# A decoder layer on one core: sample scores in four column groups, stacked rows for the compressed values, attention steps and tail without GpSimd

## The chip, the cores and the metric

The program runs on one core of a Trainium2 chip. The metric is the device time of one execution in microseconds (us), lower is better. Engines are named as in the profile: PE is TensorE (PEld its weight loads), DVE is VectorE, ACT is ScalarE, POOL is GpSimd, SP is SyncE, which issues most DMAs.

## The reference, cut to what matters

One layer of a hybrid decoder serves 256 prompt positions and 8 sample tokens together, so every linear has 264 columns. All is float32.

```python
h = rms_norm(x, norm_mix_pre)
q, kc, vc, ks, vs, kw, vw, gates, u = project(h, w_in, pos)     # rotary on the first 32 of 128 dims of q and of all keys
# three attention branches: compressed blocks, selected blocks, sliding window
kc_c, vc_c = compress(kc, *cmp_w[0]), compress(vc, *cmp_w[1])   # 15 blocks
p = masked_softmax(q @ kc_c.T * SCALE, mask);  o_cmp = p @ vc_c
o_sel, o_win = ...                                              # at this length: causal, over all keys
o = gates[..., 0:1] * o_cmp + gates[..., 1:2] * o_sel + gates[..., 2:3] * o_win
x = x + rms_norm(concat(o, pool_mix(u)) @ w_o, norm_mix_post)
x = x + rms_norm(relu(rms_norm(x, norm_mlp_pre) @ w_up) ** 2 @ w_down, norm_mlp_post)
```

The sample tokens attend to 256 cached positions each (8 sequences, paged cache rows and window rows) and to themselves.

## The kernel before, in words

Every weight matrix passes PE in three products: a weight and an activation are each split into a high part (rounded to the one-pass type, fp32r) and a low rest, and `linear` (matmul on L236) adds high x high, low x high and high x low. A weight chunk of 1 MB is loaded by SP, ACT rounds it in halves (`wh`, L195), DVE makes the rest (`wl`, L193), two halves ahead of their use. A linear runs as a series of steps; a step is six 264-column matmuls. `run` counts these steps on one clock, and the table `AT` says at which steps the parts of everything else (the named streams: rotary, scores, values, sample attention, norms) put their instructions between the linears' matmuls. So the order on every engine is written by hand, and each engine works its queue in that order.

The places that matter here lie in the second query projection (`z_q1`, steps 232 to 263) and in the first output linear (`o_pool`, from 264), up to step 333:

- `rope_part` (L500 to L503) turns the first 32 dims of two heads of a query group. `start_group` gives two of the four heads to DVE and two to POOL for the products of L501 and L503.
- `scores(g, i)` works a unit of one KV group and 128 queries: score matmuls (L805, plain fp32), a masked copy out of PSUM (L806), maxima, exponentials on ACT (L791), denominators times gates (L817 to L820), and the scaling of the three probability tiles (L824): compressed and selected ones on DVE, window ones on POOL.
- `values(g, i)` transposes the probabilities (L848) and multiplies them with the values: 128 rows at a time in three one-pass products (L208 to L210), the 16 rows of the compressed branch in one plain fp32 matmul (L841).
- `sample_attn` transposes the cached keys of each of 8 sequences (L943: four transposes for one branch and sequence), copies them out (L946 on DVE, L948 on ACT), and scores them. `score` (L932) issues two matmuls with 32 stationary columns each, one per KV group, for one branch of one sequence; they write different 32-row strips of the PSUM tile `pS`. The value product (L1002) puts eight such narrow matmuls together, over all four strips.
- `z_evac` (L490) empties the four PSUM banks of `z_q1`; `o_pool` uses these banks again, step by step.
- The tail, after the last matmul of `w_down`: squares are added up (L1175 to L1177), summed over partitions by PE (L1425), `rstd_of` takes the root in three pieces, and eight pieces of 128 x 512 outputs are formed (L1458 on DVE for six, L1451 on ACT with POOL's L1452 for two) and stored, 256 KB each; POOL also forms the sample rows.

PSUM banks for transposes and scores are two (`pmisc`, tile px), used in turn.

Of the kernel before, what the change touches and what calls it, by code (L numbers as in the profile page):

```python
# [35 lines left out]
AT = {'loads': [18], 'norm1': [31, 39, 40], 'rope_c': [38], 'rows0': [36, 37, 38, 43, 45, 48, 50, 52, 54, 58], 'heads0': [58, 59], 'rope_s': [64], 'out0': [81, 87, 92, 104], 'rows1': [106, 107, 108, 111, 114, 116, 119, 121, 124, 126], 'rope_w': [107], 'heads1': [126, 126], 'gates': [135, 136, 137, 139, 141, 142], 'v_rows': [137, 137, 143], 'out1': [161, 167, 171, 177, 178], 'diff0': [179, 180, 183, 185, 185, 186, 188], 'diff1': [204, 206, 208, 210, 212, 214, 216], 'rope_q00': [232], 'rope_q01': [230], 'scores00': [244, 244, 244, 244, 244, 244, 245, 245, 245, 245, 246], 'scores01': [243, 245, 248, 250, 250, 253, 253, 254, 255, 255, 255, 256, 257, 261], 'values00': [256, 258, 258, 258, 263, 266], 'rope_q10': [266], 'rope_q11': [264], 'values01': [265, 268, 272, 279, 279, 282, 286, 288, 291, 295], 'scores10': [279, 284, 286, 288, 290, 293, 295, 296, 299, 300, 303], 'sample': [271, 280, 280, 280, 280, 283, 285, 285, 285, 285, 286, 287, 290, 290, 290, 291, 292, 293, 294, 295, 296, 297, 298, 299, 300, 307, 311, 315, 316, 317, 319, 319, 320, 323, 323, 325, 325, 326], 'scores11': [305, 309, 310, 311, 313, 314, 315, 316, 318, 319, 320, 321, 323, 326], 'values10': [312, 319, 321, 324, 326, 327], 'values11': [327, 327, 328, 328, 329, 329, 330, 330, 331, 332], 'norm2': [424, 425, 426, 427, 428, 430, 431, 432, 435, 436, 437, 439, 440, 441, 442, 443, 447, 451, 451, 457, 459, 460, 461], 'y_rows': [456, 460, 464, 468, 472, 476, 479, 487], 'shift': [651, 655, 659, 663, 667, 671, 674, 678, 683]}  # L36
# [67 lines left out]
def nsa_pool_step(ctx: ExitStack, tc: tile.TileContext, ins, outs):  # L104
# [504 lines left out]
    def cmp_out(slot, w2s, ph):  # L609
# [156 lines left out]
    def scores(g, i, st):  # L766
# [55 lines left out]
        for j, e in enumerate((eS[:, :, 0:16], eS[:, :, 16:], eW)):  # L822
            eng = nc.gpsimd if j == 2 else nc.vector
            eng.tensor_tensor(e, e, den[:, 4 * j:4 * j + 4, None].to_broadcast([128, 4, e.shape[2]]), op=ALU.mult)  # L824

    def values(g, i, st):
        qs = slice(i * 128, (i + 1) * 128)
        eS, eW = st["eS"], st["eW"]
        parts = [(eS[:, :, 0:16], 16, [vcP[:, g, :]])]
# [15 lines left out]
        for j, (e, kw, _) in enumerate(parts):  # L845
# [22 lines left out]
    def sample_attn():  # L868
# [60 lines left out]
        def score(b, br, kt_):  # L929
            for g in range(2):  # L930
                p0 = 32 * (2 * br + g)
                nc.tensor.matmul(pS[p0:p0 + 32, 0:256], qm[:, g, 32 * b:32 * b + 32], kt_[:, g * 256:(g + 1) * 256],  # L932
                                 start=b == 0, stop=b == NB - 1)

        for b in range(NB):
            load()
            r = loaded[b]
# [422 lines left out]
    for fc in range(NFC):  # L1360
# [58 lines left out]
    parts = [acc2, last_squares(m2[:, KT - 1, :], sqs)]  # L1419
    sums = [(pacc("pP")[:, 0:1], lambda a: (a[:, 0:128], ones[:, 0:1])),  # L1420
            (pacc("pS")[:, 0:1], lambda a: (a[:, 128:256], ones[:, 0:1])),
            (pmain()[:, 0:NB], lambda a: (ones, a[:, SEQ:T]))]
# [68 lines left out]
```

## Time and profile before

| | |
|---|---|
| median of 3 runs | 1178.67 us (1178.59 to 1181.34) |
| the profiled execution's own time | 1180.37 us |
| its span, first to last instruction | 1178.6 us |
| PE busy | 1150.8 us (98%) |
| DVE, ACT, POOL busy | 689.2, 544.9, 127.9 us |
| moved by DMA | 212.09 MB, mean 180 GB/s |

The profile is of one execution. Times inside it are from the span's start. A busy PE is not a PE at its peak, since matmuls overlap: the granted clock and the distance between the starts of matmuls tell more.

### The profile page before, as it was taken

To read this page: it belongs to the slowest core of one execution; us is meant where nothing else is said; L and a number is where in the kernel's file an instruction comes from. 1 tells how busy PE (TensorE), PEld (TensorE's weight loads), DVE (VectorE), ACT (ScalarE), POOL (GpSimd) and SP (SyncE) were. 2 spreads that over 40 slices of the span, in tenths; PEclk is the share of its full clock that TensorE was granted. 3 is DMA by queue.
4 is the path that set the end of the run, shared out by engine and by line. 5 is a ranking of instruction groups with operands and counts; after the bars stand their busy time and mean duration, and the time that the engine had idled before them with its cause. 6 is when DMAs were issued, how large, how long until landed. Compare 5 with 4: busy or idle time off the path is not lost.

```text
span 1178.6 us, 22160 instructions
## 1 busy us (share of the span) xinstructions
PE 1150.8 (98%) x9303; PEld 1119.4 (95%) x9303; DVE 689.2 (58%) x970; ACT 544.9 (46%) x794; POOL 127.9 (11%) x130
## 2 busy tenths in 40 slices
PE   9999999999999999999999999999999999999996
PEld 8899999887879899999999999999999999999995
DVE  6767667874655776555445554545555445555555
ACT  6545434444446665443335543334453334444442
POOL 0121124220012464000000000000000000000211
PEclk9999999999999999999999999999999999999998
DMA  8866545445545458555555555555555555555542
GB/s 296 236 218 200 169 136 171 129 155 197 163 148 166 139 179 279 202 179 179 179 179 179 179 181 180 181 184 182 184 179 184 184 184 182 170 192 179 178 145 74
DMA packets 115789, 212.09 MB, mean 180 GB/s; under 512 B 7307, under 2 KB 23475, under 8 KB 115553
## 3 DMA queue, kind: packets, MB, share of 16 engines
q1 hardware_dynamic: 114297, 204.68, 53.4%
q0 software_dynamic: 672, 5.27, 1.3%
q8 instruction: 73, 1.20, 0.4%
q10 hardware_dynamic: 720, 0.72, 0.2%
q14 instruction: 27, 0.22, 0.1%
HBM read 206.77 MB, written 8.52 MB: 183 GB/s over the span
## 4 chain that ended last, share of the span: by engine, by line
PE 76%; DVE 3%; POOL 1%; ACT 1%; issue 1%; DVEq 0%; POOLq 0%; ACTq 0%
PE pm L236 71%; PE px L805 1%; PE pa L932 1%; PE px L943 1%; PE px L848 1%; POOL acc L1162 1%; PE pa L1002 1%; DVE orow L1458 0%; POOL xT L1260 0%; PE pa L841 0%; PE px L1333 0%; DVE h2a L1268 0%; DVE eS L824 0%; PE pa L210 0%; PE pa L209 0%
## 5 line engine op out<-in xcount | busy, mean ns | idle before, releaser
L193 DVE TENSOR_TENSOR wl<-raw,wh 128x1024 fp32r<-128x1024 f32 (+1 forms) x355 | 434.5, 1225 | 359.6 <-ACT wh L195 358.6
L195 ACT ACTIVATE wh<-raw 128x1024 fp32r<-128x1024 f32 (+1 forms) x354 | 369.2, 1048 | 463.6 <-PE pm L236 413.9
L236 PE MATMUL pm<-ah,wh 128*128 128x264 f32 x1024 | 292.0, 285 | 0.0
L236 PE MATMUL pm<-al,wh 128*128 128x264 f32 x1024 | 291.1, 284 | 0.0
L236 PE MATMUL pm<-ah,wl 128*128 128x264 f32 x1024 | 291.0, 284 | 0.0
L236 PE MATMUL pm<-h2h,wh 128*128 128x264 f32 x992 | 283.6, 286 | 0.0
L236 PE MATMUL pm<-h2h,wl 128*128 128x264 f32 x992 | 282.5, 285 | 0.0
L236 PEld LDWEIGHTS pm<-ah,wh 128*128 128x128 f32 x1024 | 193.1, 189 | 0.0
L236 PEld LDWEIGHTS pm<-al,wh 128*128 128x128 f32 x1024 | 192.8, 188 | 0.0
L236 PEld LDWEIGHTS pm<-ah,wl 128*128 128x128 f32 x1024 | 192.3, 188 | 0.0
L236 PEld LDWEIGHTS pm<-h2h,wh 128*128 128x128 f32 x992 | 187.7, 189 | 0.4 <-ACT h2h L1263 0.4
L236 PEld LDWEIGHTS pm<-h2h,wl 128*128 128x128 f32 x992 | 186.9, 188 | 0.0
L236 PE MATMUL pm<-h2b,wh 128*128 128x264 f32 x496 | 141.1, 285 | 0.5 <-DVE h2b L1268 0.5
L236 PE MATMUL pm<-h2a,wh 128*128 128x264 f32 x496 | 141.0, 285 | 0.0
L236 PE MATMUL pm<-h_hi,wh 128*128 128x264 f32 x448 | 133.0, 297 | 1.7 <-ACT wh L195 0.7
L236 PE MATMUL pm<-h_hi,wl 128*128 128x264 f32 x448 | 127.7, 285 | 1.3 <-DVE wl L193 1.2
L236 PE MATMUL pm<-h_lo,wh 128*128 128x264 f32 x448 | 127.4, 286 | 0.5 <-DVE h_lo L385 0.5
L1162 POOL TENSOR_TENSOR acc<-acc,sq 128x264 f32<-128x264 f32 x42 | 38.8, 925 | 745.2 <-ACT sq L1158 742.9
L236 PEld LDWEIGHTS pm<-h2b,wh 128*128 128x128 f32 x496 | 93.4, 188 | 0.7 <-DVE h2b L1268 0.7
L236 PEld LDWEIGHTS pm<-h2a,wh 128*128 128x128 f32 x496 | 93.6, 189 | 0.1
L236 PEld LDWEIGHTS pm<-h_hi,wh 128*128 128x128 f32 x448 | 84.8, 189 | 4.3 <-ACT wh L195 1.3
L236 PEld LDWEIGHTS pm<-h_hi,wl 128*128 128x128 f32 x448 | 84.3, 188 | 1.9 <-DVE wl L193 1.9
(573 smaller groups left out, 1396.7 us busy)
## 6 DMA issues: line engine op xcount, KB each, us to landing
raw<-in_w_up SPq DMA_DIRECT2D x64, 1024.0 KB, 5.3
raw<-in_w_down SPq DMA_DIRECT2D x64, 1024.0 KB, 5.1
raw<-in_w_in SPq DMA_DIRECT2D x25, 1024.0 KB, 5.3
raw<-in_w_o SPq DMA_DIRECT2D x16, 1024.0 KB, 5.2
rows<-in_cache_kv SPq DMA_DIRECT2D x64, 128.0 KB, 4.5
out<-in_state_win_kv POOLq DMA_DIRECT2D x8, 510.0 KB, 10.6
raw<-in_w_in SPq DMA_DIRECT2D x5, 512.0 KB, 7.7
rows<-in_state_win_kv SPq DMA_DIRECT2D x8, 256.0 KB, 5.3
```

Of the source, the lines that this page charges most:

```text
L193: eng.tensor_tensor(wl[:, a_:b_], r[:, a_:b_], wh[:, a_:b_].bitcast(F32), op=ALU.subtract)
L195: nc.scalar.activation(wh[:, a_:b_], r[:, a_:b_], AF.Copy)
L236: nc.tensor.matmul(ps[m_][:, :T], w[:, k, m_ * 128:(m_ + 1) * 128], x[:, k0 + 2 * h + k, :], start=ci == 0 and h == 0 and k == 0 and p == ...
L805: nc.tensor.matmul(pv[:, h, :], zq[g][:, h0 + h, qs], kmat, start=True, stop=True)
L848: nc.tensor.transpose(pp[:kw, h * 128:(h + 1) * 128], e[:, h, :], ident)
L932: nc.tensor.matmul(pS[p0:p0 + 32, 0:256], qm[:, g, 32 * b:32 * b + 32], kt_[:, g * 256:(g + 1) * 256], start=b == 0, stop=b == NB - 1)
L943: nc.tensor.transpose(pp[:, o:o + 128], r[:, 2 * br + c, g * 128:(g + 1) * 128], ident)
L1002: nc.tensor.matmul(po[32 * a:32 * a + 32, :128], ptm[:, a, 32 * b:32 * b + 32], r[:, 2 * (b % 2) + br, g * 128:(g + 1) * 128], start=b == ...
L1162: nc.gpsimd.tensor_tensor(a, a, sq, op=ALU.add)
```

## The change

The scores of the sample: the two branches of a sequence are scored together, so `score` issues four narrow matmuls in a row, one per strip, 8 times instead of two matmuls 16 times. A third buffer holds the transposed keys. `ptm`, the zeroed tile for the value product, now takes over `qm`'s buffer after the last score instead of having its own.

The compressed values: their rows are stacked three times to 48, with high, low and high parts of the probabilities (`ec`, made by three small DVE operations) against high, high and low parts of the values (`vcP`), so that one one-pass matmul gives the three products. For this DVE copies `hx` three times side by side (`hx3`) ahead of the matmul that makes `vcP`.

POOL leaves the attention: all query rotary goes to DVE, and the selected and window probabilities are scaled by ACT, head by head (four ACTIVATEs for a tile). The table `AT` moves places in `z_q1` and `o_pool`. The tail has no POOL work: the sums go to one bank, the root is taken once, DVE forms all eight pieces and the sample rows, and the stores are issued from SP and ACT in turn.

```diff
-AT = {... 'diff1': [204, 206, 208, 210, 212, 214, 216], 'rope_q00': [232], 'rope_q01': [230], 'scores00': [244, 244, 244, 244, 244, 244, 245, 245, 245, 245, 246], ...
+AT = {... 'diff1': [204, 206, 208, 210, 212, 214, 217], 'rope_q00': [236], 'rope_q01': [230], 'scores00': [243, 243, 243, 243, 245, 245, 245, 246, 248, 248, 248], ...
...
+            hx3 = tp.tile([128, 2, 3, 16], F32, name="hx3", tag="hx3", bufs=1)
+            nc.vector.tensor_copy(hx3, hx[:, 256:288].rearrange("p (g c) -> p g c", g=2)[:, :, None, :]
+                                  .to_broadcast([128, 2, 3, 16]))
             po = pmisc()
             for i in range(2):
-                nc.tensor.matmul(po[:16, i * 128:(i + 1) * 128], hx[:, 256 + 16 * i:272 + 16 * i], w2s,
+                nc.tensor.matmul(po[:48, i * 128:(i + 1) * 128], hx3[:, i].rearrange("p r c -> p (r c)"), w2s,
                                  start=True, stop=True)
-            nc.vector.tensor_copy(vcP, po[:16, :256].rearrange("p (a d) -> p a d", a=2))
+            pv = po[:48, :256].rearrange("p (a d) -> p a d", a=2)
+            nc.scalar.activation(vcP, pv, AF.Copy)
+            nc.vector.tensor_tensor(vcP[32:48], pv[32:48], vcP[32:48].bitcast(F32), op=ALU.subtract)
...
         for j, e in enumerate((eS[:, :, 0:16], eS[:, :, 16:], eW)):
-            eng = nc.gpsimd if j == 2 else nc.vector
-            eng.tensor_tensor(e, e, den[:, 4 * j:4 * j + 4, None].to_broadcast([128, 4, e.shape[2]]), op=ALU.mult)
+            if j:
+                for h in range(4):
+                    c = 4 * j + h
+                    nc.scalar.activation(e[:, h, :], e[:, h, :], AF.Copy, scale=den[:, c:c + 1])
+            else:
+                nc.vector.tensor_tensor(e, e, den[:, 0:4, None].to_broadcast([128, 4, 16]), op=ALU.mult)
+            if j == 0:
+                ec = ap1.tile([128, 4, 48], F32R, name="ec", tag="ec")
+                st.update(ec=ec)
+                nc.vector.tensor_copy(ec[:, :, 0:16], e)
+                nc.vector.tensor_tensor(ec[:, :, 16:32], e, ec[:, :, 0:16].bitcast(F32), op=ALU.subtract)
+                nc.vector.tensor_copy(ec[:, :, 32:48], ec[:, :, 0:16].bitcast(F32))
...
-        def score(b, br, kt_):
-            for g in range(2):
-                p0 = 32 * (2 * br + g)
+        def score(b, kts):
+            for br, kt_ in enumerate(kts):
+                for g in range(2):
+                    p0 = 32 * (2 * br + g)
...
-                if pend:
+                kts.append(kt_)
+                if br == 0 and pend:
                     score(*pend)
-                pend = (b, br, kt_)
                 yield
+            pend = (b, kts)
...
-        for k, eng in enumerate((nc.vector, nc.gpsimd)):
-            start(f"rope_q{g}{k}", rope_part(zq[g][:32, 2 * k:2 * k + 2, :], swap, eng))
+        for k in range(2):
+            start(f"rope_q{g}{k}", rope_part(zq[g][:32, 2 * k:2 * k + 2, :], swap, nc.vector))
...
-    rstd_of(rr, [o for o, _ in sums])
+    nc.vector.tensor_scalar(m2[:, last, :], m2[:, last, :], g4[:, last:KT], None, op0=ALU.mult)
+    rstd_of(rr, ss[:, 0:10])
...
+            nc.vector.scalar_tensor_tensor(o, o if a < D - 512 else last_o[i], rr[:, i:i + 1], y,
+                                           op0=ALU.mult, op1=ALU.add)
+            (nc.scalar if i else nc.sync).dma_start(y_p[0, i * 128:(i + 1) * 128, a:b], o)
```

How the order moves at three places. First, DVE's queue at the start of `z_q1`: the rotary of the first query group (zq_188), the weight rests (wl) and the first masked copies of scores (eS). Before:

```order
L193 TENSOR_TENSOR wl<-raw,wh 128x1024
L500 STREAM_SHUFFLE sw<-zq_188 32x528
L501 TENSOR_TENSOR sw<-sw,cs 32x528
L502 TENSOR_TENSOR zq_188<-zq_188,cs 32x528
L503 TENSOR_TENSOR zq_188<-zq_188,sw 32x528
L500 STREAM_SHUFFLE sw<-zq_188 32x528
L502 TENSOR_TENSOR zq_188<-zq_188,cs 32x528
L193 TENSOR_TENSOR wl<-raw,wh 128x1024 x2
L806 TENSOR_TENSOR eS<-px,cs 128x272
```

and with the change:

```order
L501 TENSOR_TENSOR sw<-sw,cs 32x528
L502 TENSOR_TENSOR zq_188<-zq_188,cs 32x528
L503 TENSOR_TENSOR zq_188<-zq_188,sw 32x528
L193 TENSOR_TENSOR wl<-raw,wh 128x1024
L500 STREAM_SHUFFLE sw<-zq_188 32x528
L501 TENSOR_TENSOR sw<-sw,cs 32x528
L502 TENSOR_TENSOR zq_188<-zq_188,cs 32x528
L503 TENSOR_TENSOR zq_188<-zq_188,sw 32x528
L193 TENSOR_TENSOR wl<-raw,wh 128x1024
L812 TENSOR_TENSOR eS<-px,cs 128x2x144 x2
```

Both pairs of heads are now turned wholly on DVE, the second pair (heads 2 and 3) first, a weight rest between them and another before the first score is copied out.

Second, DVE's queue at the end of `z_q1`, where the query banks are emptied (zq_189) and the second unit's probabilities (eS) are scaled. Before:

```order
L490 TENSOR_TENSOR zq_189<-pm,rB 128x264 x2
L817 TENSOR_REDUCE den<-eS 128x4
L818 TENSOR_SCALAR den<-den 128x12
L819 RECIPROCAL den<-den 128x12
L820 TENSOR_TENSOR den<-den,G 128x12
L824 TENSOR_TENSOR eS<-eS,den 128x4x16
L824 TENSOR_TENSOR eS<-eS,den 128x4x256
L490 TENSOR_TENSOR zq_189<-pm,rB 128x264 x2
```

and with the change:

```order
L490 TENSOR_TENSOR zq_189<-pm,rB 128x264 x2
L823 TENSOR_REDUCE den<-eS 128x4
L824 TENSOR_SCALAR den<-den 128x12
L825 RECIPROCAL den<-den 128x12
L826 TENSOR_TENSOR den<-den,G 128x12
L834 TENSOR_TENSOR eS<-eS,den 128x4x16
L839 CAST ec<-eS 128x4x16
L840 TENSOR_TENSOR ec<-eS,ec 128x4x16
L841 CAST ec<-ec 128x4x16
L490 TENSOR_TENSOR zq_189<-pm,rB 128x264
```

The wide product (4 x 256) is gone from between the emptying of the first two banks and of the third; three products or copies of 4 x 16 stand in its place.

Third, PE's queue at one place of the sample scores in `o_pool`, all between two steps of the linear. Before:

```order
L943 MATMUL px<-cs,rows 128x128 x4
L932 MATMUL pa<-kt__3370,qm 32x256 x2
L943 MATMUL px<-cs,rows 128x128 x4
L932 MATMUL pa<-kt__3428,qm 32x256 x2
L943 MATMUL px<-cs,rows 128x128 x4
L932 MATMUL pa<-kt__3437,qm 32x256 x2
```

and with the change:

```order
L962 MATMUL px<-cs,rows 128x128 x4
L950 MATMUL pa<-kt__3363,qm 32x256 x2
L950 MATMUL pa<-kt__3374,qm 32x256 x2
L962 MATMUL px<-cs,rows 128x128 x8
L950 MATMUL pa<-kt__3432,qm 32x256 x2
L950 MATMUL pa<-kt__3443,qm 32x256 x2
```

The narrow matmuls now stand in fours, behind every second group of transposes.

## Rows read from the trace of the kernel before

**Rows 1.** The page: busy time and instructions of each engine.

```profile
PE 1150.8 (98%) x9303; PEld 1119.4 (95%) x9303; DVE 689.2 (58%) x970; ACT 544.9 (46%) x794; POOL 127.9 (11%) x130
```

**Rows 2.** Busy time by stretch: length, then PE, PEld, DVE, ACT, POOL, clock, DMA.

```profile
206.49:350.04 143.55, 138.93 (x1070) 116.79 (x1068) 95.31 (x172) 65.37 (x144) 18.30 (x12) 0.98 0.48 158
220.72:224.13 3.41, 3.41 (x17) 3.19 (x15) 2.41 (x7) 1.73 (x9) 0.00 (x0) 0.50 0.70 272
248.02:251.44 3.42, 3.42 (x15) 3.13 (x15) 3.18 (x6) 0.91 (x1) 2.07 (x2) 0.50 0.02 5
```

**Rows 3.** The chain of waits in attention: start, us, what (x2 per fp32 matmul).

```profile
290.64 0.44 PE px L943 x4
291.07 0.56 PE pa L932 x4
291.63 0.93 PE pm L236 x6
...
319.15 0.57 PE pa L1002 x16
319.73 0.92 PE pm L236 x6
...
328.28 1.05 PE pa L841 x2
...
345.05 0.44 PE px L848 x4
345.49 0.73 PE pm L236 x6
```

**Rows 4.** PE in order of time: one-pass value products of 512 columns.

```profile
337.37 0.40 PE L208 MATMUL pa<-th,vparts 128*128 128x512 f32 x1
337.60 0.40 PE L209 MATMUL pa<-tl,vparts 128*128 128x512 f32 x1
```

**Rows 5.** PE and DVE in order of time, first scores.

```profile
215.26 0.62 PE L805 MATMUL px<-kx,zq 128*128 128x272 f32 x2
219.85 0.76 PE L805 MATMUL px<-kx,zq 128*128 128x144 f32 x4 [2.75 <-POOL zq L503]
...
209.76 0.76 DVE L500 STREAM_SHUFFLE sw<-zq 32x528 f32<-32x528 f32 x1
212.64 0.75 DVE L500 STREAM_SHUFFLE sw<-zq 32x528 f32<-32x528 f32 x1
```

**Rows 6.** PE and DVE in order of time, end of the query projection.

```profile
247.13 0.39 PE L236 MATMUL pm<-cc_hi,wh 128*128 128x264 f32 x1 [1.88 <-DVE zq L490]
...
243.66 3.07 DVE L824 TENSOR_TENSOR eS<-eS,den 128x64 f32<-128x64 f32 x2
```

**Rows 7.** Groups of instructions: busy, mean ns of one, idle before.

```profile
L193 DVE TENSOR_TENSOR wl<-raw,wh 128x1024 fp32r<-128x1024 f32 (+1 forms) x355 | 434.5, 1225 | 359.6 <-ACT wh L195 358.6
L791 ACT ACTIVATE eW<-eW,nmx 128x256 f32<-128x256 f32 x8 | 4.0, 497 | 3.3 <-DVE nmx L780 3.3
```

**Rows 8.** DVE in order of time: a copy of transposed keys; then value rows (also PE).

```profile
287.27 0.69 DVE L946 COPY kt__3468<-px 128x512 f32<-128x512 f32 x1 [3.07 <-PE px L943]
...
164.55 0.42 DVE L638 COPY vcR<-px 128x256 f32<-128x256 f32 x1
...
163.78 0.61 PE L642 MATMUL px<-w2t,hx 128*16 128x128 f32 x4
```

**Rows 9.** The tail: chain of waits, DVE in order of time, one stretch.

```profile
1165.42 0.44 DVE sq L1176
...
1166.80 0.73 ACT rv L450 x3
...
1168.48 5.23 DVE L1458 SCALAR_TENSOR_TENSOR orow<-orow,rr,yrow 128x512 f32<-128x512 f32 x4
1173.63 1.40 DVE L1458 SCALAR_TENSOR_TENSOR orow<-pm,rr,yrow 128x512 f32<-128x512 f32 x2
...
1174.00:1176.50 2.50, 0.00 (x0) 0.00 (x0) 1.03 (x2) 0.00 (x0) 0.00 (x0) 0.50 1.02 367
```

More of the change, by code (lines that the diff above doesn't have):

```diff
@@ L541, in nsa_pool_step @@
     vcR = zp.tile([128, 2, 128], F32, name="vcR")
-    vcP = zp.tile([16, 2, 128], F32, name="vcP")
+    vcP = zp.tile([48, 2, 128], F32R, name="vcP")
     def split(dst_h, dst_l, src):
@@ L828, in values @@
         eS, eW = st["eS"], st["eW"]
-        parts = [(eS[:, :, 0:16], 16, [vcP[:, g, :]])]
+        parts = [(st["ec"].bitcast(F32), 48, [vcP[:, g, :]])]
         for k in range(i + 1):
@@ L967, in sample_attn @@
         score(*pend)
+        ptm = ap.tile([128, 4, 288], F32, name="ptm", tag="qm", bufs=1)
+        nc.gpsimd.memset(ptm, 0.0)
         pN = pmisc()
@@ L1411, in f @@
                         later(1, lambda: add_square(acc2, m2[:, j, :], j, sqs))
-                    later(2 if j < KT - 2 else 4, gain)
+                        later(2, gain)
             return f
@@ L1416, in nsa_pool_step @@
             run(linear(downs[fc][q], ah, al, d_evac(q)))
[L1419 to L1422, printed above, removed]
+    ss = pacc("pP")
+    rr = const.tile([128, 10], F32, name="rr")
+    last = KT - 1
+    sq15 = tq.tile([128, T], F32, name="sq", tag="sq", bufs=4)
+    nc.vector.tensor_tensor(sq15, m2[:, last, :], m2[:, last, :], op=ALU.mult)
+    parts = [acc2, *sqs, sq15]
     for k, a in enumerate(parts):
-        for o, f in sums:
-            nc.tensor.matmul(o, *f(a), start=k == 0, stop=k == len(parts) - 1)
+        end = k == len(parts) - 1
+        nc.tensor.matmul(ss[:, 0:1], a[:, 0:128], ones[:, 0:1], start=k == 0, stop=end, skip_group_check=True)
+        nc.tensor.matmul(ss[:, 1:2], a[:, 128:256], ones[:, 0:1], start=False, stop=end, skip_group_check=True)
+        nc.tensor.matmul(ss[:, 2:10], ones, a[:, SEQ:T], start=False, stop=end, skip_group_check=True)
     flush()
-    rr = const.tile([128, 10], F32, name="rr")
-    rstd_of(rr, [o for o, _ in sums])
+    nc.vector.tensor_scalar(m2[:, last, :], m2[:, last, :], g4[:, last:KT], None, op0=ALU.mult)
+    rstd_of(rr, ss[:, 0:10])
     last_o = [pmain(), pmain()]
@@ L1432, in nsa_pool_step @@
             nc.tensor.transpose(last_o[i][:, k * 128:(k + 1) * 128], m2[:, KT - 4 + k, i * 128:(i + 1) * 128], ident)
-    ts = tq.tile([128, KT, NB], F32, name="ts", tag="so", bufs=2)
-    nc.gpsimd.tensor_tensor(ts, m2[:, :, SEQ:T], rr[:, None, 2:10].to_broadcast([128, KT, NB]), op=ALU.mult)
-    tt = tq.tile([128, 128], F32, name="tt", tag="t_")
-    nc.gpsimd.tensor_tensor(tt.rearrange("p (t c) -> p c t", c=KT), ts, xT[:, :, SEQ:T], op=ALU.add)
-    pp = pmisc()
-    nc.tensor.transpose(pp[:, :128], tt, ident)
@@ L1439, in nsa_pool_step @@
-    os_ = tq.tile([128, 128], F32, name="os_", tag="so", bufs=2)
-    pieces = [(i, a, b) for a, b in ((0, 512), (512, 1024), (1024, 1536), (1536, 2048)) for i in range(2)]
-    pooled = [4, 5]
-    def piece(p):
-        i, a, b = pieces[p]
-        o, y = (rows[n][:, i, a:b] for n in "oy")
-        src = o if a < D - 512 else last_o[i][:, a - D + 512:b - D + 512]
-        return o, src, y, rr[:, i:i + 1], y_p[0, i * 128:(i + 1) * 128, a:b]
-    for p in pooled:
-        o, src, y, r, _ = piece(p)
-        nc.scalar.activation(o, src, AF.Copy, scale=r)
-        nc.gpsimd.tensor_tensor(o, o, y, op=ALU.add)
```

45 lines of the change are left out of this document (25 added, 20 removed).

## The prediction

> **What bounds it now.** Start with the page: PE is busy 98% of the span, every other engine far less [rows 1]. So time is gained only by giving PE less to do, by ending its idle moments, or by a shorter tail, where PE is nearly done. Next, the windows: the attention piece from 206.49 to 350.04 lasts 143.55 us with PE busy 138.93 of it at a mean granted clock of 0.98 [rows 2]. Inside it are two stretches of 3.4 us with clock 0.50, the 1.2 GHz level; the rest stands at 2.4 GHz. Then the list in order of time, for what came ahead of each stretch: PE had waited 2.75 us for POOL's rotary (L503) at 219.85 [rows 5], and 1.88 us for DVE's emptying of a bank (L490) at 247.13 [rows 6]. Last, the chain of waits, for what a part costs that stands between two steps of a linear [rows 3]: there the cost is from start to start, the next step included, and not the part's busy time.
>
> A step without neighbours takes 0.73 us (six matmuls at 345.49), and does so behind the transposes at 345.05 [rows 3]. That is my zero.
>
> **Fewer score groups.** Transposes, a pair of narrow score matmuls and the step behind them take 0.44 + 0.56 + 0.93 = 1.93 us at 290.64; without the pair, 0.44 + 0.73 = 1.17 [rows 3]. A pair costs 0.76 us, of which 0.20 falls on the step that follows it. Eight narrow matmuls in the value product, two rounds over all four strips, take 0.57 us and lengthen the next step to 0.92 [rows 3]. So four narrow ones should cost what two do now. Sixteen pairs become eight fours: 8 x 0.76 = 6.1, taken as **-6.0**. The ends: 0 if fours cost twice a pair, and -6.1. The Trainium skill, page "TensorEngine Tiling (Array Packing)", section Key Properties, says that switching the tiling mode drains TensorE. By that rule the lengthened step belongs to each group and the sum is the one above; by the group's own 0.56 us alone it would be -4.5. The 0.93 against 0.73 agrees with the rule.
>
> **Compressed values.** L841 is plain fp32 and takes 1.05 us at 328.28 [rows 3]. One-pass products of the same 512 columns start 0.23 us apart (337.37 and 337.60 [rows 4]). One each for four units: 4 x (1.05 - 0.23) = **-3.3**; the other end is 0, if the 48-row weight load and the mode cost as much as the passes. The three small operations that make `ec` are behind the denominators, on an engine that is 95.31 us busy of 143.55 [rows 2].
>
> **First wait.** It goes with its cause: POOL no longer turns heads. Two heads take DVE 212.64 - 209.76 = 2.88 us [rows 5]. In the new order DVE does heads 2 and 3, a weight rest (1.22 us [rows 7]), heads 0 and 1: 209.76 + 2.88 + 1.22 + 2.88 = 216.7, when PE reaches its first score at about 215.3 [rows 5]. That leaves a wait of 1.4, and I add 0.5 for a masked copy behind the next weight rest: 1.9 in place of 2.75. The stretch at half clock costs half its length, 1.7 us [rows 2]. Less idle, and that split in two, I take it as gone: -(2.75 - 1.9) - 1.7 = **-2.6**. Ends: -0.9 if the clock still falls, -4.4 if nothing waits.
>
> **Second wait.** The emptying L490 stands behind L824's wide product, 3.07 us at 243.66 [rows 6]. The change sends that to ACT; three 4 x 16 operations come in its place. PE's 1.88 us and the 1.7 of the half-clock stretch after it go: **-3.6**. The banks are then free under 1 us ahead of need, so the other end is 0.
>
> **Less cutting up.** The parts now stand at 54 places between steps, before at 59; places cost what a switch does, 0.1 each: **-0.5**, between 0 and -1.
>
> **Tail.** Three DVE operations ahead of the sums (0.44 each [rows 9]) become one: -0.8. The root's three pieces on ACT (0.73 us) become one: -0.4 at most, with DVE's later steps unchanged. DVE forms all eight pieces, 8 x 0.70 (half of the 1.40 for two without POOL beside them), and the sample rows 0.6: 6.2 us, where six took 5.23 + 1.40 = 6.6 with POOL beside them. The last piece, at 1175.0 so far, comes about 1.2 to 1.6 earlier. But the DMA engines are already at a share of 1.02 there, at 367 GB/s [rows 9]; 2.1 MB of output takes 5.7 us at that rate, so the stores cannot gain more than the first one does. **-1.3**, ends 0 and -1.6. The Trainium skill, page "Trainium Kernel Development and Optimization", section Key Constraints, says that DMAs issued from several engines run on the same 16 DMA engines, and several issuers only spare issue time. By it, sharing the stores between SP and ACT gains nothing itself; the share of 1.02 agrees, and I price it at nothing.
>
> **ACT's new work.** Each of 8 scaled tiles is four ACTIVATEs; the nearest row, 128 x 256, is 497 ns [rows 7]: 32 x 0.5 = 16 us, on an engine 65.37 us busy of 143.55 [rows 2]. I price it at nothing, as long as weight rounding (L195) stays two halves, that is 8 steps or 5.8 us, ahead. If that cover is gone it is rival E.
>
> **New waits.** `hx3` stands on DVE behind the copy of value rows (164.55 + 0.42), so it ends near 165.2, while PE came to L642 at 163.78 [rows 8]: +1.4. At one place of the scores (step 287) the transposes of three sequences now stand with no step between; two px banks are used in turn, each needs a copy of 0.69 us [rows 8] against 0.44 of transposes [rows 3]: +1.2 there and +0.3 at the next place. The low parts of the probabilities at step 280 stand behind two rotaries: +0.4. The last unit's 48-row transpose goes through ACT before its product: +0.3. Value rows are loaded closer together: +0.6. First transposes of each unit wait for ACT's scaling: +0.3. Together **+4.5**, between 0 (each estimate covered) and +8.
>
> **Sum.** -6.0 - 3.3 - 2.6 - 3.6 - 0.5 - 1.3 + 4.5 = -12.8. The profiled execution took 1180.37 us, 1.7 above the median of 1178.67; it would come to 1167.6, and the median to **1165.9 us**.
>
> **Rivals.**
> A, the forecast: 1165.9. Chance 0.64.
> B, the waits move and do not go. For: DVE gets POOL's rotary, and PE still waits 1.4 + 0.5 at the first score; the margin at the second place is under 1 us. Against: both causes leave. Without the 2.6 and 3.6 the sum is -6.6: 1172.1. Chance 0.20.
> C, no new waits: the estimates of +4.5 find cover in work that shifts earlier with the gains. Sum -17.3: 1161.4. Against: the wait at `hx3` is read from two rows. Chance 0.08.
> D, the change does not do what it says: fours do not run together, each costs two pairs. Without the 6.0, -6.8: 1171.9. For: no row shows scores of 256 columns on four strips. Against: the eight narrow matmuls in 0.57 us. Chance 0.04.
> E, slower. ACT works its queue in order, and two blocks of four ACTIVATEs per unit put 8 x 0.5 = 4 us ahead of a weight rounding; DVE's rest of it (1.22 us) follows. It decides when the rounding that PE needs next stands behind a block and less than 4 us ahead. Then PE loses about 3 us at each of four units and falls to half clock each time: 4 x (3 + 1.7) = 18.8, sum +6.0: 1184.7. Against: the lead of 5.8 us, and the idle before L193 is already put down to waiting for L195 [rows 7] with no loss on PE. Chance 0.04.
>
> **The numbers.** About 0.3%, 3.5 us, is what a measurement of this kernel can tell from no change. A, C and D lie beyond that on the fast side, and B in part: 6.6 less another miss of 3 is "same". So faster 0.90, same 0.06, slower 0.04. The range goes from 1161.0 (C) to 1172.5 (B and D, with some tenths); outside are E, deeper mixes of B and D, and the gain ends of several terms at once.
>
> **What would show it.** A group of four scores near 0.57 us and L858's product near 0.25 in PE's list; a wait of some 1.4 and 0.5 us at the first scores with no clock of 0.50 behind it; none at the end of the query projection; a wait of 1.4 us at the `vcP` product near 164; no POOL work in the attention; the last piece about 1.2 us earlier. The forecast is wrong if the stretches at 0.50 stay, if groups of four take 1.1 us, if ACT's scaling stands ahead of a rounding that PE waits for, or if new waits together pass 8 us.

## The result, and the profile after

| | before | changed |
|---|---|---|
| median, 6 runs each | 1180.57 us (1178.59 to 1181.70) | 1169.71 us (1168.04 to 1170.59) |
| ratio of the times | | 0.9909, 95% interval 0.9896 to 0.9922 |
| span of the profiled execution | 1178.6 us | 1167.7 us |

The change is faster by 10.7 us (9.2 to 12.3). The forecast was 12.8, and 1165.9 us in a range of 1161.0 to 1172.5; the time is inside it, 3.8 above the forecast, of which 1.9 is the base (1180.57 here, 1178.67 before).

Busy time of the engines in the changed kernel, the page's first part (before: [rows 1]):

```profile
PE 1142.2 (98%) x9311; PEld 1117.9 (96%) x9311; DVE 684.5 (59%) x982; ACT 554.2 (47%) x824; POOL 107.3 (9%) x118
```

PE is still the bound. The rest of the reading needs one ruler. Both kernels send the same 8256 matmuls of L236 through PE, so the time between the starts of two of them, counted in steps of six from the first, can be compared stretch by stretch:

| steps (us in the kernel before) | before | changed | difference |
|---|---|---|---|
| 146 to 150 (163 to 167): value rows | 4.17 | 5.60 | +1.43 |
| 203 to 293 (214 to 350): attention | 135.50 | 122.56 | -12.94 |
| 351 to 420: second norm | 68.30 | 69.56 | +1.26 |
| from the last one to the end: tail | 14.54 | 14.13 | -0.41 |

All other stretches differ by 0.2 in sum. Two of the four differences are partly the clock's. Attention before held two stretches at clock 0.50 [rows 2] and now holds none, -3.4; the one at 401.6 us before is gone, and another stands at 439.3 us now, behind a wait of 2.2 us for POOL's sum that stands in both kernels and had no fall behind it before; with no fall ahead of it, a wait of 1.1 us for `h2a` shows at 393.6, which is most of the +1.26. So without the falls attention went from 132.1 to 122.6, by 9.5 us. (The run with the new tail alone, further down, has the old attention and no fall in it: 132.43 us.)

What PE waits for in the attention of the changed kernel (the list of waits from 200 to 350 us: engine, tile and line, releaser, us in total, times, longest):

```profile
PE px L811 <- DVE zq L503: 1.2, 1, 1.2
PE px L962 <- DVE kt__3347 L965: 0.5, 1, 0.5
PE px L962 <- DMA rows<-in_cache_kv: 0.4, 1, 0.4
PE px L811 <- DVE eS L812: 0.3, 1, 0.3
PE pa L858 <- ACT th L868: 0.2, 1, 0.2
PE pa L1024 <- DVE ptm L1014: 0.2, 1, 0.2
```

The two waits of before (2.75 in [rows 5], 1.88 in [rows 6]) have become 1.2 and nothing, and five small ones, 1.6 together, are new. These are the forecast's 1.4, its 0.5 (here 0.3), and its list of new waits.

A place with one group of four scores, and one product of the stacked rows (PE in order of time):

```profile
278.42 0.60 PE L962 MATMUL px<-cs,rows 128*128 128x128 f32 x4
278.95 0.41 PE L950 MATMUL pa<-kt__3454,qm 128*32 128x256 f32 x2
278.96 0.41 PE L950 MATMUL pa<-kt__3471,qm 128*32 128x256 f32 x2
279.19 0.39 PE L950 MATMUL pa<-kt__3454,qm 128*32 128x256 f32 x2
279.20 0.39 PE L950 MATMUL pa<-kt__3471,qm 128*32 128x256 f32 x2
279.52 0.39 PE L236 MATMUL pm<-cc_hi,wh 128*128 128x264 f32 x1
...
235.78 0.50 PE L858 MATMUL pa<-th,vcP 48*128 48x512 f32 x1
236.21 0.66 PE L865 MATMUL px<-cs,eS 128*128 128x128 f32 x4
```

The four strips do run together: two matmuls start 10 ns apart, and the group takes 279.52 - 278.95 = 0.57 us, what the pair took [rows 3]. The stacked product takes 236.21 - 235.78 = 0.43 us from start to start, not the 0.23 that I had read from products of 128 rows [rows 4].

The copy of `hx` in the way of the `vcP` product (the chain of waits, 162 to 166 us):

```profile
162.00 2.35 DVE wl L193 x2
164.36 0.33 DVE vcR L638
164.69 0.13 DVE hx L642
```

and PE's own line:

```profile
164.95 0.61 PE L646 MATMUL px<-w2t,hx 128*48 128x128 f32 x4 [1.36 <-DVE hx L642]
```

PE had been free since 163.6, so it waits 1.36 us; the forecast said 1.4, from DVE's copy in [rows 8].

The tail (the chain of waits), and ahead of it the last linear matmul of the kernel before (PE in order of time):

```profile
1164.06 0.28 PE L236 MATMUL pm<-ah,wl 128*128 128x264 f32 x1
```

```profile
1153.90 0.13 PE pa L1451 x2
...
1156.32 0.45 PE pa L1453 x2
...
1156.79 0.28 ACT rv L450
...
1158.03 1.41 DVE orow L1464 x2
```

From the end of the linear at 1153.9 to the root's first step at 1156.79, 2.9 us, there is no wait: PE works through four parts with three sums each. Before there were two parts, the second after three DVE operations, and the root began at 1166.80 [rows 9], 2.5 us after the linear's end at 1164.34. The shorter root, 1.24 us to the first piece in place of 1.68 [rows 9], only makes up for that: the first output piece starts 4.1 us after the linear in both kernels. What DVE saved, PE now spends.

### The profile page after: what moved, and what is told of

Read it like the earlier page. It is cut to its first block, busy times and chain, and to the rows that moved or that the text cites. A ratio compares the mean times of both kernels' runs of the same rounds, so it can differ in the third digit from the quotient of the medians.

```text
span 1167.7 us, 22184 instructions
## 1 busy us (share of the span) xinstructions
PE 1142.2 (98%) x9311; PEld 1117.9 (96%) x9311; DVE 684.5 (59%) x982; ACT 554.2 (47%) x824; POOL 107.3 (9%) x118
## 4 chain that ended last, share of the span: by engine, by line
PE 87%; DVE 5%; DMA 3%; ACT 2%; issue 1%; POOL 1%; SPq 1%; DVEq 0%; ACTq 0%; POOLq 0%
PE pm L236 79%; DVE wl L193 2%; ACT wh L195 1%; DMA raw<-in_w_in 1%; PE pa L209 1%; PE pa L208 1%; PE pa L210 1%; PE px L811 1%; DMA rows<-in_cache_kv 1%; PE px L578 1%; PE px L962 1%; POOL acc L1182 1%; POOL xT L1280 1%; PE px L865 0%; DMA raw<-in_w_o 0%
## 5 line engine op out<-in xcount | busy, mean ns | idle before, releaser
L193 DVE TENSOR_TENSOR wl<-raw,wh 128x1024 fp32r<-128x1024 f32 (+1 forms) x355 | 434.0, 1223 | 363.4 <-ACT wh L195 362.6
L195 ACT ACTIVATE wh<-raw 128x1024 fp32r<-128x1024 f32 (+1 forms) x354 | 369.3, 1048 | 450.6 <-PE pm L236 413.3
L236 PE MATMUL pm<-ah,wh 128*128 128x264 f32 x1024 | 292.0, 285 | 0.0
L236 PE MATMUL pm<-al,wh 128*128 128x264 f32 x1024 | 291.1, 284 | 0.0
L236 PE MATMUL pm<-ah,wl 128*128 128x264 f32 x1024 | 291.0, 284 | 0.0
L236 PE MATMUL pm<-h2h,wh 128*128 128x264 f32 x992 | 283.6, 286 | 0.2 <-ACT h2h L1283 0.2
L236 PE MATMUL pm<-h2h,wl 128*128 128x264 f32 x992 | 282.6, 285 | 0.0
L236 PEld LDWEIGHTS pm<-ah,wh 128*128 128x128 f32 x1024 | 193.1, 189 | 0.0
L236 PEld LDWEIGHTS pm<-al,wh 128*128 128x128 f32 x1024 | 192.7, 188 | 0.0
L236 PEld LDWEIGHTS pm<-ah,wl 128*128 128x128 f32 x1024 | 192.3, 188 | 0.0
L236 PEld LDWEIGHTS pm<-h2h,wh 128*128 128x128 f32 x992 | 187.8, 189 | 0.5 <-ACT h2h L1283 0.5
L236 PEld LDWEIGHTS pm<-h2h,wl 128*128 128x128 f32 x992 | 187.1, 189 | 0.0
L236 PE MATMUL pm<-h2b,wh 128*128 128x264 f32 x496 | 141.9, 286 | 0.5 <-DVE h2b L1288 0.5
L236 PE MATMUL pm<-h2a,wh 128*128 128x264 f32 x496 | 140.6, 284 | 1.1 <-DVE h2a L1288 1.1
L236 PE MATMUL pm<-h_hi,wh 128*128 128x264 f32 x448 | 132.5, 296 | 1.1 <-DVE h_hi L426 0.5
L236 PE MATMUL pm<-h_hi,wl 128*128 128x264 f32 x448 | 127.5, 285 | 1.4 <-DVE wl L193 1.4
L236 PE MATMUL pm<-h_lo,wh 128*128 128x264 f32 x448 | 127.2, 285 | 0.5 <-DVE h_lo L385 0.5
L236 PEld LDWEIGHTS pm<-h2b,wh 128*128 128x128 f32 x496 | 94.1, 190 | 0.7 <-DVE h2b L1288 0.7
L236 PEld LDWEIGHTS pm<-h2a,wh 128*128 128x128 f32 x496 | 93.2, 188 | 1.3 <-DVE h2a L1288 1.3
L236 PEld LDWEIGHTS pm<-h_hi,wh 128*128 128x128 f32 x448 | 84.5, 189 | 3.5 <-ACT h_hi L381 0.7
L236 PEld LDWEIGHTS pm<-h_hi,wl 128*128 128x128 f32 x448 | 84.2, 188 | 2.0 <-DVE wl L193 2.0
```

Of the source, the lines that this page charges most:

```text
L193: eng.tensor_tensor(wl[:, a_:b_], r[:, a_:b_], wh[:, a_:b_].bitcast(F32), op=ALU.subtract)
L195: nc.scalar.activation(wh[:, a_:b_], r[:, a_:b_], AF.Copy)
L236: nc.tensor.matmul(ps[m_][:, :T], w[:, k, m_ * 128:(m_ + 1) * 128], x[:, k0 + 2 * h + k, :], start=ci == 0 and h == 0 and k == 0 and p == ...
```

## Experiments

Each kernel stands against the kernel before on the same chip, the difference in us being the ratio's on that median. Three groups: single parts in the kernel before, all parts or all places alone, and the changed kernel with one thing taken back. My theory after the result was the forecast's sum, with the falls of the clock set too high; the rivals were that the parts do not earn their price one by one, and that the places do.

**Score groups alone**, in the kernel before.

```diff
-                kt_ = ap1.tile([128, 512], F32, name="kt_", tag="pT", bufs=2)
+                kt_ = ap1.tile([128, 512], F32, name="kt_", tag="pT", bufs=3)
...
-                if pend:
+                kts.append(kt_)
+                if br == 0 and pend:
                     score(*pend)
```

> The kernel before with the score groups of four alone (third buffer for the transposed keys, ptm in qm's buffer), old places. My reading of the changed kernel's trace (group 0.57 us, neighbours as for a pair): 8 groups fewer at 0.76 us, -6.0 us, in a bound of -4.5 to -6. If four strips do not run together (rival D): 0 to +6 us. PE's list should show the group near 0.57 us and the step behind it 0.8 to 0.95.

Measured: 0.9953 (0.9937 to 0.9970), -5.5 us. Between steps 241 and 258, where all scores but the last stand, and free of falls in both, the kernel is 4.4 us shorter. Step by step: the six steps that lose a pair take 0.72 or 0.73 less each (1.92 to 1.20 in one), 4.35 in all. At the other two places three pairs became two fours with no step between them, and there one group less saves 0.5 and 0.3, not 0.72: 5.1 together. Waits of 0.5 for a copy and 0.3 for rows take 0.8 back. Another 1.3 us goes behind the scores, most of it in one step of the value product that waits for rows; that step takes 2.7 to 4.0 us in the six other traces with the old places and 4.35 here, so it is not shown to be the groups' doing. Rival D is out.

**Stacked rows alone.**

```diff
-    vcP = zp.tile([16, 2, 128], F32, name="vcP")
+    vcP = zp.tile([48, 2, 128], F32R, name="vcP")
...
+            if j == 0:
+                ec = ap1.tile([128, 4, 48], F32R, name="ec", tag="ec")
...
-        return ap1.tile([128, 2, T], F32, name="sw", tag="sw", bufs=1)[:32]
+        return ap1.tile([128, 2, T], F32, name="sw", tag="pT", bufs=2)[:32]
```

> The kernel before with the 48 stacked rows alone (hx3, ec, one-pass product), old places, GpSimd kept; the rotary's scratch tile shares the buffers of the transposed keys for space. By the prediction's prices: 4 x (1.05 - 0.23) less 1.4 for the wait on hx3 = -1.9 us. By the changed kernel's trace, where the product takes 0.43: 4 x (1.05 - 0.43) - 1.2 = -1.3 us. If the wait on hx3 does not show, -2.5 us.

Measured: 1.0052 (1.0035 to 1.0068), 6.1 us slower: no expectation had that sign. DVE and PE in order of time say why:

```profile
244.63 0.23 DVE L830 TENSOR_TENSOR eS<-eS,den 128x64 f32<-128x64 f32 x1
244.89 3.29 DVE L835 CAST ec<-eS 128x64 fp32r<-128x64 f32 x1
248.22 0.23 DVE L836 TENSOR_TENSOR ec<-eS,ec 128x64 fp32r<-128x64 f32 x1
248.37 0.19 DVE L837 CAST ec<-ec 128x64 fp32r<-128x64 f32 x1
...
248.70 1.02 PE L861 MATMUL px<-cs,ec 128*48 128x128 f32 x4 [3.47 <-DVE ec L837]
```

The same cast in the changed kernel:

```profile
227.86 0.20 DVE L839 CAST ec<-eS 128x64 fp32r<-128x64 f32 x1
```

A cast of 0.20 us took 3.29, and PE stood 3.47 us behind it. POOL, in the run with the stacked rows, was scaling the window probabilities and zeroing `qm` and `ptm` from 244.7 to 248.1:

```profile
244.73 1.90 POOL L830 TENSOR_TENSOR eW<-eW,den 128x1024 f32<-128x1024 f32 x1 [15.60 <-ACT wh L195]
246.57 0.58 POOL L1132 MEMSET qm<- 128x576 f32 x1
247.08 1.06 POOL L1134 MEMSET ptm<- 128x1152 f32 x1
```

DVE and POOL hold each other up, and the forecast had no term for it. The cast ends at 248.2, as POOL's last memset does. It was there to be read in the kernel before: DVE's L824 took 3.07 us [rows 6], beside this on POOL.

```profile
243.76 1.90 POOL L824 TENSOR_TENSOR eW<-eW,den 128x1024 f32<-128x1024 f32 x1 [15.12 <-ACT wh L195]
```

DVE's L824 is two products there, a short one and the wide one; the wide one began at 243.80, 0.04 us behind POOL's. In the run with the score groups it began at 243.37, 0.04 us ahead of POOL's, and DVE had the way (DVE, then POOL):

```profile
243.23 1.36 DVE L824 TENSOR_TENSOR eS<-eS,den 128x64 f32<-128x64 f32 x2
244.50 0.77 DVE L490 TENSOR_TENSOR zq<-pm,rB 128x264 f32<-128x264 f32 x2
245.19 2.23 DVE L193 TENSOR_TENSOR wl<-raw,wh 128x1024 fp32r<-128x1024 f32 x1
...
243.41 2.93 POOL L824 TENSOR_TENSOR eW<-eW,den 128x1024 f32<-128x1024 f32 x1 [14.84 <-ACT wh L195]
```

There L824 took 1.36, POOL 2.93 in place of 1.90, and PE's wait of 1.88 us was gone, though the edit touches neither L824 nor L490. So 1.9 of that run's -5.5 is this, and not the groups.

The Trainium skill, page "SBUF — State Buffer", section "Who interferes with whom", says that a VectorE instruction with two inputs in SBUF contends with a GpSimd instruction that reads SBUF, since they share a port pair, and that one holds it until it is done. By that rule the loser's time grows by what is left of the winner's, and the four rows agree to 0.2 us: 1.36 + 1.7 for DVE against POOL's 1.90, or 1.90 + 1.0 for POOL against the 1.2 that were left of DVE's product. Why the cast, which has one input, is held too, no row shows.

The product itself saves what its new length says: the four steps that hold it are 0.61 or 0.62 us shorter each than in the kernel before. The loss lies around it.

**POOL out of the attention alone**, in the kernel before.

```diff
-        for k, eng in enumerate((nc.vector, nc.gpsimd)):
+        for k in range(2):
...
-            eng = nc.gpsimd if j == 2 else nc.vector
+            if j:
+                for h in range(4):
+                    c = 4 * j + h
+                    nc.scalar.activation(e[:, h, :], e[:, h, :], AF.Copy, scale=den[:, c:c + 1])
```

> The kernel before with POOL out of the attention alone: rotary on DVE, selected and window probabilities scaled by ACT; old places, old scores, old values. If the engines alone end the two waits: -6.2 us (2.6 + 3.6) and no stretch at clock 0.50 near 220 and 248 us. If the places of the table are what ends them (the waits move to DVE's queue): between -2 and +2 us, with waits over 1.5 us left at the first scores. If ACT's blocks hold up the weight rounding: over +5 us.

Measured: 1.0035 (1.0020 to 1.0050), 4.1 us slower. Both old waits are gone: at the first scores PE waits 0.25 us for a copy and 0.54 for a weight rest, where it waited 2.75 for POOL. Others came. ACT, DVE and PE in order of time:

```profile
225.15 2.46 ACT L826 ACTIVATE eS<-eS,den 128x128 f32<-128x128 f32 x8 [0.77 <-DVE den L820]
227.51 1.99 ACT L195 ACTIVATE wh<-raw 128x1024 fp32r<-128x1024 f32 x2
...
228.59 1.23 DVE L193 TENSOR_TENSOR wl<-raw,wh 128x1024 fp32r<-128x1024 f32 x1 [3.27 <-ACT wh L195]
229.73 0.78 DVE L806 TENSOR_TENSOR eS<-px,cs 128x272 f32<-128x272 f32 x2
...
230.22 1.13 PE L805 MATMUL px<-zw,zq 128*128 128x256 f32 x4 [1.02 <-DVE eS L806]
```

ACT's block of eight stands ahead of the rounding (L195), DVE's rest of the weight (L193) waits 3.27 us for it, the score copies queue behind that, and PE waits for the copies. This is rival E's mechanism with another last link: not the weight, but the copy behind it. The same place in the changed kernel:

```profile
224.30 1.06 ACT L195 ACTIVATE wh<-raw 128x1024 fp32r<-128x1024 f32 x1 [1.09 <-issue]
...
225.39 1.23 DVE L193 TENSOR_TENSOR wl<-raw,wh 128x1024 fp32r<-128x1024 f32 x1 [0.72 <-ACT wh L195]
...
227.66 2.45 ACT L832 ACTIVATE eS<-eS,den 128x128 f32<-128x128 f32 x8 [0.76 <-DVE den L826]
```

A rounding and its rest stand ahead of the block, and nobody waits for what follows.

**Scaling on ACT alone** splits that run: of its diff the second part, the rotary left as before.

> The kernel before with the scaling of selected and window probabilities on ACT alone; rotary still on POOL, old places. It halves the run without GpSimd (+4.1 us). If ACT's blocks of 2.4 to 3.4 us ahead of a weight rounding are what cost there: +2 to +5 us, with DVE's L193 waiting over 2 us for L195 near 228 us and PE for DVE's score copies. If the moved rotary was the cost: -2 to -4 us, the wait at 245 us gone.

Measured: 1.0040 (1.0025 to 1.0055), 4.7 us slower, with PE waits of 1.6 and 1.4 for score copies and 1.4 for L193. So ACT's blocks, with what queues behind them, are the cost.

**Tail alone**: the last hunk of the change (the sums in one bank, L1446 on) in the kernel before.

> The kernel before with the new tail alone. By the prediction: -1.3 us, mostly because the root comes 0.8 us earlier. By the changed kernel's trace, where the first output piece starts as long after the last linear matmul as before (4.3 us) and the last store ends 0.4 us earlier by the same measure: -0.4 us. If the bytes of the stores set the end: 0.

Measured: 0.9996 (0.9984 to 1.0009), -0.5 us and not to be told from nothing. From the last matmul of the linears to the end it takes 13.87 us, 14.54 before.

**All parts in the old places**: the changed kernel with the old table.

```diff
-AT = {... 'rope_q00': [236], ... 'scores00': [243, 243, 243, 243, 245, ...
+AT = {... 'rope_q00': [232], ... 'scores00': [244, 244, 244, 244, 244, ...
```

> The changed kernel with the old table of places: all its parts, none of its new order. Against the kernel before: if the places are what lets the parts pay (the three parts measured alone sum to -5.5 + 6.1 + 4.1 = +5 us), 0 to +8 us, with waits of PE for DVE's copies and for the small probabilities as in those runs. If the parts help each other (no GpSimd, so no wide product between the parts of the stacked rows), -5 to -9 us.

Measured: 0.9986 (0.9972 to 1.0000), -1.7 us, between the two expectations. The single parts sum to -5.5 + 6.1 + 4.1 - 0.5 = +4.2; together they do better by 6. That is no sign that the parts help each other. The stacked rows' cast takes 0.20 us without POOL, but two of the single parts end the same wait, so that at step 225, where both stand, the single parts sum to -1.5 us and this run has -1.6 (each against the run with the new tail, which has the old attention and no fall in it). Much of the 6 is falls of the clock that the profiled runs of single parts had in the attention, 3.4 us by the ruler, and 2.1 in a step that waits for rows. PE still waits 2.8 us for score copies, 1.4 for window copies and 1.4 for DVE's rests of the output parts, the waits of the two runs with ACT's blocks in the old places.

**New places alone**: the same line the other way round, in the kernel before.

> The kernel before with the new table of places alone. If the new order is good in itself: -3 to -6 us. If it is cut to the new parts and does nothing for the old ones: -1 to +5 us, since POOL's rotary (L503, done at 219.8 us) and DVE's wide product are as late as before while the first scores now stand one step earlier.

Measured: 0.9988 (0.9978 to 0.9998), -1.4 us. The first scores still wait, 2.4 us. DVE, then POOL:

```profile
215.25 0.73 DVE L500 STREAM_SHUFFLE sw<-zq 32x528 f32<-32x528 f32 x1
...
210.92 2.91 POOL L501 TENSOR_TENSOR sw<-sw,cs 32x528 f32<-32x528 f32 x1 [8.37 <-issue]
213.90 1.31 POOL L503 TENSOR_TENSOR zq<-zq,sw 32x528 f32<-32x528 f32 x1
```

POOL's pair now comes first, and DVE's shuffle cannot start before POOL's L503 ends at 215.2, for there is one buffer for `sw`.

**Scratch copy earlier.** The changed kernel with `hx3` copied a step sooner:

```diff
         nc.vector.tensor_tensor(hx, hx, hu, op=ALU.mult)
+        if slot:
+            hx3 = tp.tile([128, 2, 3, 16], F32, name="hx3", tag="hx3", bufs=1)
+            nc.vector.tensor_copy(hx3, ...)
         yield
```

> The changed kernel with hx3 copied right behind the product that makes hx, a step earlier. The wait of 1.33 us at the vcP product near 164 us should go: 1.2 to 1.4 us less than the changed kernel, so -12 us against the kernel before. If another wait takes its place (w2 or the copy of value rows): no difference from the changed kernel, -10.7.

Measured: 0.9888 (0.9867 to 0.9908), -13.2 us. The interval overlaps the changed kernel's, but the trace has it plainly: steps 146 to 150 take 4.20 us again (5.60 in the changed kernel), with no wait at L646.

**The changed kernel without the stacked rows.**

```diff
-        parts = [(st["ec"].bitcast(F32), 48, [vcP[:, g, :]])]
+        parts = [(eS[:, :, 0:16], 16, [vcP[:, g, :]])]
```

> The changed kernel with the compressed values as before: 16 rows, the plain fp32 product, no hx3, no ec. By the prediction's terms the stacked rows earn 3.3 and cost 1.4 and 0.3: the run is 1.6 us slower than the changed kernel, -9.1 us against the kernel before. By the product's measured 0.43 us, they earn 2.5 and cost 1.3: 1.2 slower, -9.5. If they cost as much as in the run where they stood alone (+6.1), the run is faster than the changed kernel by some us, -13 or less.

Measured: 0.9899 (0.9877 to 0.9921), -11.9 us: not slower than the changed kernel, as far as can be measured. By the ruler it gains 1.41 us at steps 146 to 150 and loses 1.0 in the attention, where neither has a fall. The steps say more. The four that hold the product are 0.61 to 0.63 longer each, 2.5 in all (1.66 to 2.28 in the first). Against that two steps that wait for cached rows (256 and 285) are 0.65 and 0.66 shorter here. They vary without any change to the attention, too: in the run with the early copy they take 3.05 and 4.74, in the changed kernel 3.68 and 3.62. So the stacked rows earn 2.5 us at their products and pay 1.4 for `hx3`; whether the waits for rows are theirs as well, one trace does not tell.

**The changed kernel with POOL's half of the rotary.**

```diff
-            start(f"rope_q{g}{k}", rope_part(zq[g][:32, 2 * k:2 * k + 2, :], swap, nc.vector))
+            start(f"rope_q{g}{k}", rope_part(zq[g][:32, 2 * k:2 * k + 2, :], swap, eng))
```

> The changed kernel with the rotary of heads 2 and 3 of each group back on POOL. The prediction gave the move 0.85 us of wait and 1.7 of clock, 2.6 together: -8.1 us against the kernel before. If POOL's rotary was late only because of the old order: no difference, -10.7. If the new order, with the first scores a step earlier, is cut to DVE: 3 to 6 us slower than the changed kernel, with a wait over 2.5 us at the first scores.

Measured: 0.9907 (0.9885 to 0.9930), -11.0 us, no difference. PE, then DVE:

```profile
218.56 0.64 PE L811 MATMUL px<-kx,zq 128*128 128x144 f32 x3 [1.30 <-DVE zq L503]
...
215.96 1.82 DVE L502 TENSOR_TENSOR zq<-zq,cs 32x528 f32<-32x528 f32 x1
```

The wait at the first scores is 1.30 us, 1.17 in the changed kernel, although POOL turns two heads again: with three buffers for `sw` POOL and DVE overlap, and they slow each other (1.82 us where a lone one takes 0.69). So the wait of 2.75 came from POOL's pair standing second, behind DVE's queue and one buffer. There are two ways out of it: to take POOL out, as in the old places (0.25 and 0.54), or to put its pair first with three buffers (1.30). New places with one buffer (2.4) or two buffers in the old places (2.7, in the run with the stacked rows) do not end it.

**The changed kernel with the scaling as before.**

```diff
-            if j:
-                for h in range(4):
...
+            eng = nc.gpsimd if j == 2 else nc.vector
+            eng.tensor_tensor(e, e, den[:, 4 * j:4 * j + 4, None].to_broadcast([128, 4, e.shape[2]]), op=ALU.mult)
```

> The changed kernel with selected probabilities scaled by DVE and window ones by POOL, as before. The prediction gave this move 3.6 us: -7.1 us against the kernel before. In the old order ACT's scaling cost 4.7 us, so if the new order only takes that cost away: no difference, -10.7. If DVE's wide product and POOL's hold each other up again (DVE's 3.07 us at 243.7 against 1.36 in another run): a wait of 1.5 to 4 us at the end of the query projection, and -4 to -8.

Measured: 0.9981 (0.9967 to 0.9996), -2.2 us (-3.9 to -0.5): 8.5 of the 10.7 us are gone, more than any theory gave. The list of PE's waits from 200 to 350 us, and DVE and POOL beside each other:

```profile
PE px L861 <- DVE ec L837: 1.9, 1, 1.9
PE px L1032 <- DVE o L1029: 1.6, 1, 1.6
PE px L811 <- DVE zq L503: 1.2, 1, 1.2
PE px L861 <- DVE eW L812: 0.9, 1, 0.9
PE px L861 <- DVE eS L812: 0.8, 1, 0.8
```

```profile
245.26 2.33 DVE L835 CAST ec<-eS 128x64 fp32r<-128x64 f32 x1
...
245.14 1.89 POOL L830 TENSOR_TENSOR eW<-eW,den 128x1024 f32<-128x1024 f32 x1 [13.98 <-DVE den L826]
246.97 0.58 POOL L1137 MEMSET qm<- 128x576 f32 x1
```

The cast is held up once more, 2.33 us for 0.20, to the end of POOL's memset, and DVE's wide products make the copies behind them late. Attention takes 129.35 us, 122.56 in the changed kernel, with no fall in either: 6.8 us. The run keeps the stacked rows, so the held-up cast is part of that price; what the scaling costs without them was not measured.

**Early copy, and first scores a step later.**

```diff
-AT = {... 'scores00': [243, 243, 243, 243, 245, 245, 245, 246, 248, 248, 248], ...
+AT = {... 'scores00': [244, 244, 244, 244, 245, 245, 245, 246, 248, 248, 248], ...
```

> The changed kernel with hx3 copied early and the first four places of the first scores one step later. The wait of 1.17 us for DVE's rotary near 216 us should fall by about a step, 0.7 us: 1.3 + 0.7 = 2.0 us less than the changed kernel, -12.7 against the kernel before. If the score copies now stand behind a weight rest: 0 to 1 us given back.

Measured: 0.9891 (0.9869 to 0.9913), -12.9 us, and the wait at the first scores is still 1.18. The edit missed its target: the unit that waits is `scores01`, whose first place is also 243 and was not moved. Steps 203 to 206 take 0.35 us less, which the times do not show, so the early copy alone is as good. Those two kernels, at -13.2 and -12.9, are the fastest here, ahead of the changed kernel by the 1.4 us that the trace shows, a difference that the times do not resolve.

## Why the prediction was right, and where it was not

| term of the sum | forecast | what the runs showed |
|---|---|---|
| score groups | -6.0 | -5.1, with two waits that come with them -4.3 |
| stacked rows, with `hx3` and the 48-row transpose | -3.3 + 1.4 + 0.3 = -1.6 | -2.5 at the products, +1.4 for `hx3`: -1.1 (+0.4 with the waits for rows beside them in one trace) |
| first wait | -0.85 | -1.3 (2.75 to 1.17 and 0.26) |
| second wait | -1.9 | -1.9, the wait is gone; to put the scaling back costs 6.8 in the attention |
| falls of the clock behind the two waits | -3.4 | none left in five traces; before, two in one trace and none in another |
| less cutting up | -0.5 | not measured by itself (before, a step behind transposes takes 0.81 us, others 0.73) |
| other new waits in the attention | +2.8 | +1.4 (0.5, 0.4, 0.2, 0.2) |
| tail | -1.3 | -0.4; alone -0.7 by its trace, -0.5 by its times |
| second norm | 0 | +1.26 in the profiled execution |

The direction, the bound and the two places were right: PE bound, two waits leave, the group of four costs what the pair cost, `hx3` costs 1.36 where 1.4 was said, and the first scores wait 1.17 and 0.26 for 1.4 and 0.5. By stretches the forecast was -12.9 in the attention, +1.4 at the value rows and -1.3 in the tail; the traces show -12.94, +1.43 and -0.41, and +1.26 in the second norm. The miss of 1.9 between the two spans is therefore the tail, 0.9, and the second norm, for which the forecast had nothing. That one is a draw: the stretch takes 68.0 to 68.3 us in the six traces whose only fall there comes at step 352, and 69.5 to 71.3 in the eight with a fall at step 408 or 409; the run with the new tail alone took 71.27 with the same second norm as the kernel before, 68.30.

That the attention came out to 0.1 us is luck. The groups were priced 0.9 too high, the stacked rows' products 0.8 and the new waits 1.4, and these errors cancel for the most part. Five steps did not hold as they were written.

**The clock.** "The stretch at half clock costs half its length" and "I take it as gone" made of one execution a rule for all. In the five traces with the new attention no stretch at 0.50 stands in it, and so far it came true. But the run with the new tail has the old attention and the same waits, 2.7 and 1.9 us, and no fall there; it fell for 6.8 us at 447 instead. Its attention takes 132.43 us, that of the kernel before, with two falls, 135.50. So the term was worth 3.1 us in one execution and nothing in another, and how often the kernel before falls there is open. The mean clock of the runs does not settle it, since it counts the tail, too, where the clock stood at 0.50 for 9.0 us of the span before and for 11.7 in the changed kernel.

**Score groups.** "8 x 0.76" took each group to have a step of its own behind it. Two of the eight stand where three pairs stood with no step between, and save 0.5 and 0.3.

**Second wait.** The cause, "L490 stands behind L824's wide product, 3.07 us", was half read: the two products of L824 take 1.36 us, the rest is POOL holding them up. The wait went as forecast, but what the scaling's move is worth in the changed kernel, 6.8 us, lies in waits that the forecast did not see. The cover named for ACT ("weight rounding (L195) stays two halves, that is 8 steps or 5.8 us, ahead") holds in the new places and not in the old, where ACT's scaling costs 4.7 us. Rival E got 0.04; its mechanism is real, with blocks of 2.46 us in place of 4, and the table of places is what keeps it off. What the forecast put down to parts is a matter of parts and places together: -1.7 and -1.4 alone, -10.7 together.

**Stacked rows.** "One-pass products of the same 512 columns start 0.23 us apart" was taken from products of 128 rows; this one takes 0.43. And the three small operations were "on an engine that is 95.31 us busy of 143.55", which says nothing of POOL beside them.

**Tail.** "Three DVE operations ahead of the sums (0.44 each [rows 9]) become one: -0.8" forgot PE's own work on four parts instead of two: the sums end 2.9 us after the last linear matmul, 2.5 before.

The first wait was priced well, and its cause, "POOL no longer turns heads", is enough by the run without POOL. It is not needed in the changed kernel: with POOL's rotary back the wait is 1.30, as three buffers and the new places end it, too.

## What to carry to other kernels

Before an instruction's time is priced as its own, look for the same instruction elsewhere and at what DVE and POOL do beside it: a 0.20 us cast at 3.29 us is a wait in disguise. In a queue order written by hand, parts and places are one change: taken one by one they can point the wrong way. A fall of the clock that one trace shows can be a draw: look for it in a second execution with the same waits before pricing it.

## What the runs showed of the hardware that I had not expected

DVE and POOL delay each other for whole instructions, whichever comes first: L824 3.07 or 1.36 us, POOL's product 1.90 or 2.93, a cast 0.20, 2.33 or 3.29. Both long casts end within 0.05 us of the end of what POOL was doing, the memsets behind its product included.

The spread between runs of the kernel before and of the run with the new tail goes with the mean granted clock. Of the 18 runs of the kernel before the fastest, 1178.51 us, had 0.995 and the slowest, 1184.15 us, 0.989; of 12 with the new tail, 1176.81 us at 0.995 and 1183.12 us at 0.989. One stretch of 3.41 us at 0.50 is 1.7 us, or 0.0014 of the mean clock. Which of the waits brings one differs from execution to execution; why, these runs leave open.

Two matmuls of 32 stationary columns for two strips cost as much as four for four strips, 0.57 us with 256 columns each.
